# A two-layer hybrid block: paired chunks, masks folded into a matmul, and one convolution tile moved to the end of its section

## The chip, the cores and the metric

The kernel runs on one core of one Trainium2 chip. The metric is device time in microseconds (us) of one execution. The profiled execution is one such run with the hardware profiler on; its span (first to last instruction) is what the rows of a profile add up to.

## What is computed

Two layers over 256 context and 1024 latent tokens of width 1024, one batch. Each layer makes a combined input projection and runs three groups of heads: a bidirectional state-space scan (16 heads of 64, state 128, chunks of 128 tokens), windowed attention, and a convolution module with 31 taps on 512 channels. The change touches the first and the third.

```python
# state space, one direction (the other runs on reversed tokens)
cs = cumsum(dt * a)                       # per chunk of 128 tokens and head
decay = exp(where(tril, cs[l] - cs[s], -inf))
y_diag = (C B^T * decay) @ (x * dt)       # inside a chunk
states = B^T (decay_to_end * x * dt)      # carried from chunk to chunk
y = y_diag + exp(cs) * (C @ entering_state) + D * x
...
# convolution module
h = val * sigmoid(gt)
h = dwconv_31(h)                          # per channel, 31 taps, along the tokens
h = silu(layernorm(h)) @ pw_w
```

## The kernel before

All sequence work is kept as columns: a tile has 128 channels on its partitions and tokens along its free axis. There are ten chunks of 128 tokens, two of context (0, 1) and eight latent (2 to 9). A layer is `ssd_section` (projections for state space and convolution, the scan, the taps), then `att_section`, then `out_section`. The large projections (`gemm1`, tiles `pj`) multiply each weight tile three times, for high and low parts of both operands; they are most of the work of TensorE (PE). The build step orders every engine's queue by a timeline of its own, so a queue runs in a fixed order and each instruction waits at its head.

The scan of a layer is four calls of `half(i, xk)`, each for four heads in both directions. A half has ten steps; step `si` takes the forward chunk `cf` and the backward chunk `cb`, updates the state `S`, and `visit`s each chunk. A chunk's second visit calls `diag(c)`, which makes the decay weights of both directions: the exponents come from matmuls `pc` (forward part and off-diagonal blocks) and `pd` (backward part of the two diagonal 64 by 64 blocks) of `L` (cumulative sums split in three bf16 terms, as rows) with `R` (selectors of heads, and three rows that a DMA brings from `csd`). Triangular masks are added by further matmuls of `identb` with `mask_lt` or `mask_gt`. ScalarE (ACT) takes exponentials into `ex` and `eb`, GpSimd (POOL) adds `eb` into the diagonal blocks of `ex`, VectorE (DVE) multiplies by `cbs`, and PE multiplies `xk` with the result in the same bank in which the chunk's `yp` was transposed; ACT moves the sum out as `yT`. In layer 1 the context chunks have no output, so a half has eight second visits there and ten in layer 0: 72 in all.

Between halves, `conv_gemm(i)` projects convolution channel tile `i` into `gl`; its function `taps` runs `conv31` (one ACT instruction and 30 on DVE for each block of tokens, tile `ua`, result `u`) or, for blocks in `LATER`, stores `gl` to DRAM for the attention section. The rows of `L` are made once per layer before the first half from the tile `qq`.

Of the kernel before, what the change touches and what calls it, by code (L numbers as in the profile page):

```python
# [19 lines left out]
P = 128  # L20
# [35 lines left out]
LATER = (((3, 0), (3, 256), (3, 768)), ((3, 256), (3, 768)))  # L56
STQ = "scalar"
EARLY = 1
SHARE = ((1, 3, 5, 7), (1, 3, 5, 7))
NSM = 4  # L60
# [8 lines left out]
def build(tc, A, out, stop=None, dbg=None):  # L69
# [56 lines left out]
    sel_c = cp.tile([P, 16], BF16, name="sel_c")  # L126
    sel4 = cp.tile([P, 32], F32, name="sel4")
    nc.vector.tensor_reduce(out=sel4[:, 0:16], in_=ident[:, 0:96].rearrange("p (a b) -> p b a", b=16), axis=mybir.AxisListType.X, op=ALU.add)
    nc.vector.tensor_copy(out=sel_c, in_=sel4[:, 0:16])
# [14 lines left out]
    csd = [dp.tile([2, 3, 2, 2, 4, T], BF16, name=f"cs{l}") for l in range(DEPTH)]  # L144
# [401 lines left out]
    def ssd_section(l, last, early):  # L546
        v1 = vec1[l]
        gblocks = LATB if last else ALLB
        with ExitStack() as st:
# [11 lines left out]

            w = load_dt(l)
# [122 lines left out]
            def d1(name, keep=False, dt_=F32):  # L685
                if keep:
                    return sp.tile([P, NCH * 32], F32, tag=name, name=name)
                t = sp.tile([P, 512], dt_, tag="xk", name=name, bufs=7)
                return t[:, 0:NCH * 32]
# [50 lines left out]


            nc.vector.tensor_scalar_mul(out=cs, in0=cs, scalar1=-1.0)
            L = []
            for g in range(2):
                qq = sp.tile([P, NCH, P], BF16, tag=("cbs", "btok")[g], name="qq")
# [4 lines left out]
                for c0, t in ((0, cs), (48, ld)):  # L750
                    x = v4(v3(t))[:, :, :, 8 * g:8 * g + 8]
                    q = [v4(qq[:, :, c0 + 16 * k:c0 + 16 * k + 16]) for k in range(3)]
                    nc.vector.tensor_copy(out=q[0], in_=x)
                    nc.vector.tensor_tensor(out=x, in0=x, in1=q[0], op=ALU.subtract)
                    nc.vector.tensor_copy(out=q[1], in_=x)
                    nc.vector.tensor_tensor(out=q[2], in0=x, in1=q[1], op=ALU.subtract)
                nc.gpsimd.memset(qq[:, :, 96:P], -1.0)
                lt = sp.tile([P, T], BF16, tag=f"L{g}", name="L")
                for b0 in range(0, NCH, 4):
                    nb = min(4, NCH - b0)  # L760
                    pr = pp.tile([P, 1024], BF16, tag="sm", name="pr", bufs=NSM)
                    for c in range(b0, b0 + nb):
# [192 lines left out]
            for i in range(4):  # L955
# [6 lines left out]
                if i == 1:  # L962
                    bc_group(1)
# [524 lines left out]
```

## Time and profile before

| what | value |
|---|---|
| median of 3 runs (lowest to highest) | 2394.25 us (2392.6 to 2397.82) |
| the profiled execution's own time | 2391.2 us |
| its span | 2389.5 us, 36713 instructions |
| PE busy | 2286.8 us, 96% |
| DVE, ACT, POOL busy | 1528.7, 990.3, 1074.5 us |
| granted TensorE clock, mean | 0.985 |

A busy figure is the time in which at least one instruction of the engine was under way. Matmuls overlap at their ends, so PE's work is read from the distance between starts, not from durations. Of the span, the first state-space section takes about 140 to 620 us and the second about 1380 to 1800 us.

### The profile page before, as it was taken

The page shows a single profiled execution, that of the slowest core. Times are in us where ns is not written, and L with a number is a line of the kernel's source. Part 1 is how long each engine was busy: PE and PEld are TensorE (multiplying, and loading weights), DVE is VectorE, ACT ScalarE, POOL GpSimd, SP SyncE. Part 2 cuts the span into 40 slices and gives each one's busy share as a digit, 9 for nine tenths or more (in the row PEclk, how much of TensorE's full clock was granted, in tenths as well). Part 3 has the DMA queues.
Part 4 walks back from the last instruction along what each step waited for, and adds up shares of the span by engine and source line. Part 5 has one row for each costly group of instructions (what it writes and reads, how often), then busy time and mean ns, then how long its engine had stood idle before and what let it go on. Part 6 is the DMA issues. An engine that isn't in the chain of part 4 may idle for free.

```text
span 2389.5 us, 36713 instructions
## 1 busy us (share of the span) xinstructions
PE 2286.8 (96%) x13237; PEld 1813.4 (76%) x13237; DVE 1528.7 (64%) x2738; ACT 990.3 (41%) x2141; POOL 1074.5 (45%) x1249
## 2 busy tenths in 40 slices
PE   6999999999999999999999999999989899998998
PEld 3787678677878777767888787778768676776798
DVE  5779899941266756657363779969323865866534
ACT  6643243322236454544243443343222354554433
POOL 4237663764454323422333346756575532512333
PEclk9999999999999999999999999999999999999999
DMA  7412312333124222247465211111222313226563
GB/s 235 147 59 86 89 49 65 85 101 111 36 83 116 66 72 80 63 152 240 143 201 151 75 41 54 32 41 45 81 54 58 106 58 98 75 71 184 179 177 110
DMA packets 324246, 237.04 MB, mean 99 GB/s; under 512 B 56066, under 2 KB 280546, under 8 KB 324064
## 3 DMA queue, kind: packets, MB, share of 16 engines
q1 hardware_dynamic: 280832, 193.28, 27.5%
q10 hardware_dynamic: 42336, 41.06, 5.5%
q8 instruction: 104, 1.70, 0.3%
q0 software_dynamic: 896, 0.35, 0.1%
q14 instruction: 78, 0.64, 0.1%
HBM read 181.63 MB, written 53.00 MB: 98 GB/s over the span
## 4 chain that ended last, share of the span: by engine, by line
PE 77%; DVE 9%; DMA 6%; ACT 2%; POOL 2%; issue 2%; SPq 1%; ACTq 0%; DVEq 0%; POOLq 0%
PE pj L97 54%; PE sm L97 6%; PE s L97 4%; PE o L97 3%; PE pt L1094 3%; DVE us L513 3%; PE po L97 2%; DMA raw<-oT 2%; PE pc L97 1%; PE pm L97 1%; DMA wr<-w_out 1%; DMA wm<-w_mod 1%; PE sm L917 1%; DVE acc L601 1%; SPq L292 1%
## 5 line engine op out<-in xcount | busy, mean ns | idle before, releaser
L97 PE MATMUL pj<-hh,wh 128*128 128x512 f32 (+1 forms) x1840 | 693.9, 378 | 11.4 <-DVE kb L999 3.3
L97 PE MATMUL pj<-hl,wh 128*128 128x512 f32 (+1 forms) x1840 | 687.2, 373 | 1.6 <-POOL hl L204 1.6
L97 PE MATMUL pj<-hh,wl 128*128 128x512 f32 (+1 forms) x1840 | 686.9, 374 | 1.5 <-POOL wl L423 1.4
L423 POOL TENSOR_TENSOR wl<-wr,wh 128x512 fp32r<-128x512 f32 x268 | 358.1, 1339 | 491.0 <-ACT wh L421 467.0
L97 PEld LDWEIGHTS pj<-hh,wh 128*128 128x128 f32 x1840 | 350.3, 190 | 80.6 <-issue 10.6
L97 PEld LDWEIGHTS pj<-hh,wl 128*128 128x128 f32 x1840 | 349.6, 190 | 61.8 <-issue 6.3
L97 PEld LDWEIGHTS pj<-hl,wh 128*128 128x128 f32 x1840 | 350.5, 191 | 59.8 <-issue 6.8
L421 ACT ACTIVATE wh<-wr 128x512 fp32r<-128x512 f32 x344 | 215.8, 630 | 377.5 <-PE pj L97 288.9
L513 DVE SCALAR_TENSOR_TENSOR ua<-gl,vec,ua 128x512 f32<-128x512 f32 (+1 forms) x435 | 303.2, 697 | 12.0 <-ACT ua L511 5.4
L601 DVE SCALAR_TENSOR_TENSOR acc<-raw,vec,acc 128x514 f32<-128x514 f32 (+2 forms) x280 | 190.4, 692 | 24.2 <-ACT acc L598 22.6
L97 PE MATMUL pj<-ho,wh 128*128 128x256 f32 (+1 forms) x896 | 179.1, 299 | 0.0
L97 PE MATMUL pj<-hx,wh 128*128 128x512 f32 x512 | 166.3, 406 | 10.5 <-DVE hx L505 4.8
L97 PEld LDWEIGHTS pj<-ho,wh 128*128 128x128 f32 x896 | 143.9, 191 | 5.5 <-ACT wh L421 0.2
L938 POOL TENSOR_TENSOR xs<-xk,ws 128x256 f32<-128x256 f32 x144 | 90.4, 639 | 123.2 <-PE sm L97 106.6
L898 POOL TENSOR_TENSOR ex<-ex,eb 64x256 f32<-64x256 f32 x144 | 114.8, 797 | 58.6 <-ACT eb L896 51.4
L1084 ACT ACTIVATE p<-s,sums 128x512 f32<-128x512 f32 (+1 forms) x144 | 95.0, 660 | 102.9 <-DVE sums L1082 82.4
L513 DVE SCALAR_TENSOR_TENSOR us<-gl,vec,us 128x512 f32<-128x512 f32 (+1 forms) x150 | 131.5, 877 | 6.2 <-ACT us L511 4.0
L97 PE MATMUL pj<-ho,wl 128*128 128x256 f32 (+1 forms) x448 | 134.5, 300 | 0.5 <-POOL wl L423 0.3
L1081 DVE TENSOR_REDUCE mx<-s 128x1 f32<-128x512 f32 (+1 forms) x144 | 93.2, 654 | 55.4 <-PE s L97 54.8
L97 PEld LDWEIGHTS pj<-hx,wh 128*128 128x128 f32 x512 | 99.5, 195 | 35.7 <-DVE hx L505 7.2
L912 POOL TENSOR_TENSOR yp<-yp,ye 128x256 f32<-128x256 f32 x136 | 103.3, 776 | 26.8 <-DVE ye L911 26.5
L1094 PE MATMUL pt<-ident,p 128*128 128x128 f32 x640 | 104.0, 278 | 11.7 <-ACT p L1084 7.1
(326 smaller groups left out, 3920.8 us busy)
## 6 DMA issues: line engine op xcount, KB each, us to landing
wr<-w_in SPq DMA_DIRECT2D x160, 256.0 KB
wr<-w_out SPq DMA_DIRECT2D x114, 256.0 KB
wm<-w_mod SPq DMA_DIRECT2D x64, 256.0 KB
raw<-oT ACTq DMA_DIRECT2D x64, 256.0 KB
wr<-w_out SPq DMA_DIRECT2D x76, 128.0 KB
yT<-yT ACTq DMA_DIRECT2D x72, 128.0 KB
wm<-w_mod SPq DMA_DIRECT2D x16, 512.0 KB
wr<-w_in SPq DMA_DIRECT2D x64, 128.0 KB
```

The source lines that it names most:

```text
L97: return nc.tensor.matmul(o, l, r, start=start, stop=stop)
L292: nc.sync.dma_start(out=wm, in_=A["w_mod"][0].rearrange("(k p) c -> p k c", p=P)[:, k:k + 8 // WD, m * P:(m + WD) * P])
L421: nc.scalar.activation(out=hi, in_=raw, func=AF.Copy)
L423: low_eng[0].tensor_tensor(out=lo, in0=raw, in1=f32(hi), op=ALU.subtract)
L513: nc.vector.scalar_tensor_tensor(out=u if t == 30 else acc, in0=g[:, t:t + n], scalar=vec2[l][:, t, j:j + 1], in1=acc, op0=ALU.mult, op1=A ...
L601: nc.vector.scalar_tensor_tensor(out=acc, in0=raw[:, i0 + t:i0 + t + n], scalar=v1[:, cw:cw + 1], in1=acc, op0=ALU.mult, op1=ALU.add)
L898: nc.gpsimd.tensor_tensor(out=e[q, :, q], in0=e[q, :, q], in1=eb[q], op=ALU.add)
L912: nc.gpsimd.tensor_tensor(out=y, in0=y, in1=ye, op=ALU.add)
L938: nc.gpsimd.tensor_tensor(out=h3(xs), in0=xc(c), in1=hb(ws3, c, d), op=ALU.mult)
L1081: nc.vector.tensor_reduce(out=mx, in_=s, axis=mybir.AxisListType.X, op=ALU.min)
L1084: nc.scalar.activation(out=flat(p[:, 0:min(nk, 4), :]), in_=s, func=AF.Exp, scale=-1.0, bias=nm[:, j:j + 1], accum_out=sums[:, 3, j:j + 1])
L1094: last_t[:] = [nc.tensor.transpose(pt[:, q * P:(q + 1) * P], pr[q][:, i, :], ident)]
```

## The change

It has these parts:

- **Masks in the matmul.** `L` gets an identity block in its partitions 64 to 127 and `R` the masks in the same partitions, so one matmul over 128 rows gives a masked exponent. `R` has three versions of its selectors, `pc` is two matmuls of 512 columns, `pd` two of 256, and no mask matmul is left. The fixed parts of `R` and `L` are written by POOL at the start of the section; each half rewrites the selectors with four ACT instructions for each of two `R`.
- **Two chunks at a time.** `diag` becomes `weights(cc)` and `outputs(cc, e)`: both chunks of a step share `ex`, `eb`, `pd`, the transposed bank and `yT`. `outputs` of one pair and `weights` of the next are tied in PE's order by `issue_after`. `ex`, `eb` and `yT` have one buffer where they had two.
- **Scaling of the carried part on ACT.** `ye`, one DVE instruction of 256 columns, becomes four ACT instructions of 64 columns.
- **Rows.** `L` and `csd` are made by `rows()` after `inputs(0)`, five chunks at a time, with 24 small DMAs to `csd` in place of 4, and one `R` load of a chunk in place of two.
- **TAIL.** The taps of channel tile 1 no longer run after `inputs(2)`: `gl` is stored to DRAM, and `tail_taps` loads it again and runs the taps at the end of the section.

```diff
+TAIL = 1
...
+            Rs = []
+            for _ in range(2):
+                R = sp.tile([P, 3, 4, P], BF16, tag="R", name="R", bufs=2)
+                nc.gpsimd.memset(R[32:64], 0.0)
+                nc.gpsimd.memset(R[64:P, 0:2], 0.0)
+                for v, t0, m in ((0, 0, mask_lt), (1, 64, mask_lt), (2, 0, mask_gt), (2, 64, mask_gt)):
+                    nc.gpsimd.tensor_copy(out=R[64:P, v, :, t0:t0 + 64], in_=m[64:P, 64:P].unsqueeze(1).to_broadcast([64, 4, 64]))
+                Rs.append(R)
...
+                        if j == TAIL or (j, off) in LATER[l]:
                             nc.sync.dma_start(out=glTd[l][:, j, u0:u0 + n + 30], in_=gl[:, u0:u0 + n + 30])
...
+            def tail_taps():
+
+                gl = ra("gt")
+                for a, b in ([] if last else [(0, 286)]) + [(286, RA)]:
+                    nc.sync.dma_start(out=gl[:, a:b], in_=glTd[l][:, TAIL, a:b])
+                for off, n in gblocks:
+                    u0 = off if off < CTX else off + 30
+                    conv_taps(TAIL, off, n, gl[:, u0:u0 + n + 30])
...
-                Rs = []
-                for _ in range(2):
-                    R = sp.tile([P, 2, 4, P], BF16, tag="R", name="R", bufs=2)
-                    nc.vector.tensor_copy(out=R, in_=sel4(sel_c).unsqueeze(3).to_broadcast([P, 2, 4, P]))
-                    Rs.append(R)
+                for R in Rs:
+                    for v, d, t0, t1 in ((0, 0, 0, P), (2, 1, 0, P), (1, 1, 0, 64), (1, 0, 64, P)):
+                        nc.scalar.activation(out=R[0:48, v, :, t0:t1], in_=sel_c[0:48, d, 4 * hf:4 * hf + 4].unsqueeze(2).to_broadcast([48, 4, t1 - t0]), func=AF.Copy)
...
-                    mm(pc[:, :, qs[1]], lt[0:99, c * P:(c + 1) * P], r0[:, :, qs[1]], start=True, stop=False)
-                    mm(pc[qs[0], :, qs[0]], ll[0], r0[:, :, qs[0]], start=False, stop=False)
-                    mm(pc[qs[1], :, qs[0]], ll[1], r1[:, :, qs[0]], start=False, stop=False)
+                    with after(last_mm):
+                        for u, (R, c) in enumerate(zip(Rs, cc)):
+                            ll = [lt[:, c * P + a:c * P + a + 64] for a in (0, 64)]
+                            pc = pp.tile([P, 4, P], F32, tag="sm", name="pc", bufs=NSM)
+                            for v, (q, lq) in enumerate(zip(qs, ll)):
+                                mm(pc[q], lq, R[:, v])
+                            for q, lq in zip(qs, ll):
+                                mm(pd[q, u], lq, R[:, 2, :, q])
+                            pcs.append(pc)
+                    for u in range(2):
+                        nc.scalar.activation(out=flat(e[:, u]), in_=flat(pcs[u]), func=AF.Exp)
+                    nc.scalar.activation(out=eb, in_=pd, func=AF.Exp)
                     for q in qs:
-                        mm(pc[q, :, q], identb[:, q], mask_lt[:, q].unsqueeze(1).to_broadcast([P, 4, 64]), start=False, stop=True)
...
-                        mm(pc[q], identb[:, q], mask_gt[:, q].unsqueeze(1).to_broadcast([P, 4, 64]), start=False, stop=True)
...
-                        nc.gpsimd.tensor_tensor(out=e[q, :, q], in0=e[q, :, q], in1=eb[q], op=ALU.add)
+                        nc.gpsimd.tensor_tensor(out=e[q, :, :, q], in0=e[q, :, :, q], in1=eb[q], op=ALU.add)
+                    for u, c in enumerate(cc):
+                        nc.vector.tensor_tensor(out=e[:, u], in0=e[:, u], in1=cbs[:, c, :].unsqueeze(1).to_broadcast([P, 4, P]), op=ALU.mult)
...
-                        nc.vector.tensor_tensor(out=h3(ye), in0=h3(yo), in1=hb(ecs3, c, d), op=ALU.mult)
+                        for h in range(4):
+                            k = 16 * d + H0 + h
+                            nc.scalar.activation(out=ye[:, h * 64:(h + 1) * 64], in_=yo[:, h * 64:(h + 1) * 64], func=AF.Copy, scale=ecs3[:, c, k:k + 1])
...
+                    if si == 2 and not last:
+                        e = weights(steps[1])
+                    if si == 3:
+                        if not last:
+                            outputs(steps[1], e)
+                        e = weights(steps[6])
+                    if si > 6:
+                        outputs(steps[si - 1], e)
+                        e = weights(steps[si])
+                outputs(steps[9], e)
...
+            tail_taps()
             for r in range(NAG[l]):
                 gate_gemm(r)
```

How the queues change is shown at three places. First PE's queue, where one chunk's weights stand in layer 0 before the change (`pc` and `pd` are the exponents, `identb` the mask matmuls; LDWEIGHTS rows are weight loads):

```order
L97 LDWEIGHTS identb
L97 MATMUL pc<-mask_lt,identb 64x4x64
L97 LDWEIGHTS L
L97 MATMUL pd<-R,L 64x4x64
L97 LDWEIGHTS L
L97 MATMUL pd<-R,L 64x4x64
L97 LDWEIGHTS identb
L97 MATMUL pd<-mask_gt,identb 64x4x64
L97 LDWEIGHTS identb
L97 MATMUL pd<-mask_gt,identb 64x4x64
L97 MATMUL pj<-hl_1006,wh 128x512
```

After it, a pair's outputs (`sm<-ex,xk`, two chunks), the next pair's weights behind them, and what PE has until the outputs of that pair; these are the last two pairs of the last half of layer 1 (the rows between `pc` and the second `pd` of the first pair are left away here, they repeat those shown):

```order
L98 MATMUL pd<-R,L 64x256
L98 MATMUL pj<-hh_12695,wl 128x512
L98 MATMUL sm<-S,ct 128x256 x2
L952 MATMUL sm<-ident,yp 128x128 x4
L98 MATMUL sm<-ex,xk 64x128 x8
L98 LDWEIGHTS L
L98 MATMUL pc<-R,L 64x512
L98 LDWEIGHTS L
L98 MATMUL pc<-R,L 64x512
```

```order
L98 MATMUL pd<-R,L 64x256
L952 MATMUL sm<-ident,yp 128x128 x4
L98 MATMUL sm<-ex,xk 64x128 x8
L98 LDWEIGHTS nident
L98 MATMUL s_18483<-mask_gt,nident 128x512
L98 MATMUL pj<-hh_12092,wh 128x512
```

A pair has four `pc` and four `pd` rows and no mask row; `nident` and the `pj` rows behind it belong to the attention section. Between the weights of a pair and its outputs stand here one projection matmul, two of `S` and the transposes, and for the last pair the transposes alone.

DVE's queue at the end of the state-space section of layer 0, after the change (`ua<-gt` are taps of the moved tile, `S` the state update, `ex<-ex,cbs` the multiplication of the weights):

```order
L515 SCALAR_TENSOR_TENSOR ua<-gt,vec_0_391,ua 128x512 x10
L931 TENSOR_TENSOR ex<-ex,cbs 128x512 x2
L515 SCALAR_TENSOR_TENSOR ua<-gt,vec_0_391,ua 128x512
L984 TENSOR_TENSOR S<-S,sm 128x512
L515 SCALAR_TENSOR_TENSOR ua<-gt,vec_0_391,ua 128x512 x9
L931 TENSOR_TENSOR ex<-ex,cbs 128x512 x2
L515 SCALAR_TENSOR_TENSOR ua<-gt,vec_0_391,ua 128x512 x6
L515 SCALAR_TENSOR_TENSOR u<-gt,vec_0_391,ua 128x512
```

Before, this part of DVE's queue holds no taps: only `ye`, `S` and `ex` rows follow each other there. Now the last tap stands ahead of the last pair's `ex` rows.

## Rows read from the trace of the kernel before

**Rows 1.** The page: busy time by engine, and the chain that ended last.

```profile
PE 2286.8 (96%) x13237; PEld 1813.4 (76%) x13237; DVE 1528.7 (64%) x2738; ACT 990.3 (41%) x2141; POOL 1074.5 (45%) x1249
...
PE 77%; DVE 9%; DMA 6%; ACT 2%; POOL 2%; issue 2%; SPq 1%; ACTq 0%; DVEq 0%; POOLq 0%
```

**Rows 2.** Stretches: length, busy PE, PEld, DVE, ACT, POOL, clock, DMA share.

```profile
60.00:95.00 35.00, 32.63 (x175) 27.17 (x175) 24.93 (x48) 24.87 (x53) 7.96 (x16) 0.94 0.58 203
140.00:510.00 370.00, 360.46 (x2311) 279.37 (x2304) 319.89 (x559) 133.63 (x287) 225.71 (x336) 1.00 0.26 75
510.00:620.00 110.00, 103.15 (x618) 79.00 (x617) 30.24 (x58) 30.38 (x62) 58.44 (x71) 0.97 0.33 93
1320.00:1350.00 30.00, 25.82 (x129) 21.48 (x128) 19.66 (x38) 15.63 (x26) 11.15 (x17) 0.89 0.31 97
...
1520.00:1570.00 50.00, 42.60 (x241) 32.62 (x242) 46.64 (x80) 13.20 (x27) 38.87 (x54) 0.93 0.11 30
...
1700.00:1770.00 70.00, 70.00 (x363) 57.28 (x362) 11.77 (x22) 15.91 (x34) 44.81 (x63) 1.00 0.27 77
1770.00:1805.00 35.00, 27.36 (x194) 19.29 (x193) 15.48 (x29) 13.91 (x31) 23.72 (x28) 0.95 0.25 73
```

**Rows 3.** Timeline of PE, one chunk's weights: start, length, instruction.

```profile
302.73 0.51 PE L97 MATMUL pc<-R,L 99*128 99x256 bf16 x3
303.07 0.28 PE L97 MATMUL pc<-mask_lt,identb 128*64 128x256 bf16 x2
303.18 0.28 PE L97 MATMUL pd<-R,L 99*64 99x256 bf16 x2
...
303.50 0.50 PE L97 MATMUL pj<-hh,wh 128*128 128x512 f32 x1
```

**Rows 4.** Timeline of PE: outputs of one chunk alone.

```profile
311.02 0.66 PE L97 MATMUL sm<-ex,xk 128*64 128x128 f32 x8
311.60 0.39 PE L97 MATMUL pj<-hl,wh 128*128 128x256 f32 x1
```

**Rows 5.** Timeline of PE: outputs of two chunks in a row, between projections.

```profile
343.90 0.39 PE L97 MATMUL pj<-hl,wh 128*128 128x512 f32 x1
344.13 0.39 PE L97 MATMUL pj<-hh,wl 128*128 128x512 f32 x1
344.45 1.09 PE L97 MATMUL sm<-ex,xk 128*64 128x128 f32 x16
345.47 0.50 PE L97 MATMUL pj<-hh,wh 128*128 128x512 f32 x1
```

**Rows 6.** Groups by line, shapes apart, of ACT, POOL and DVE: busy, mean ns.

```profile
L889 ACT ACTIVATE ex<-pc 128x512 f32<-128x512 f32 x72 | 43.0, 597 | 104.1 <-PE pd L97 45.4 <-PE pc L97 32.4 <-DMA R<-cs 8.1
...
L1113 ACT ACTIVATE sums<-sums 128x8 f32<-128x8 f32 x18 | 3.8, 209 | 0.4 <-DVE sums L1112 0.4
...
L423 POOL TENSOR_TENSOR wl<-wr,wh 128x512 fp32r<-128x512 f32 x268 | 358.1, 1339 | 491.0 <-ACT wh L421 467.0 <-DMA xb<-xT 8.6 <-DMA wr<-w_out 5.2
...
L513 DVE SCALAR_TENSOR_TENSOR ua<-gl,vec,ua 128x512 f32<-128x512 f32 x348 | 260.8, 750 | 8.5 <-ACT ua L511 4.1
...
L911 DVE TENSOR_TENSOR ye<-sm,ecs 128x256 f32<-128x256 f32 x136 | 51.2, 416 | 65.0 <-PE sm L97 64.8 <-POOL yp L912 0.2
...
L513 DVE SCALAR_TENSOR_TENSOR ua<-gl,vec,ua 128x256 f32<-128x256 f32 x87 | 42.4, 487 | 3.5 <-ACT ua L511 1.3
```

**Rows 7.** Timeline of all engines: the last chunk of layer 1's last half.

```profile
1786.21 0.52 PE L97 MATMUL pc<-R,L 99*128 99x256 bf16 x3
...
1787.37 0.38 ACT L896 ACTIVATE eb<-pd 128x256 f32<-128x256 f32 x1
...
1787.83 1.62 POOL L898 TENSOR_TENSOR ex<-ex,eb 64x256 f32<-64x256 f32 x2 [0.46 <-ACT eb L896]
...
1789.49 0.69 DVE L900 TENSOR_TENSOR ex<-ex,cbs 128x512 f32<-128x512 f32 x1 [1.40 <-POOL ex L898]
...
1790.23 0.33 PE L97 MATMUL sm<-ex,xk 128*64 128x128 f32 x2 [1.43 <-DVE ex L900]
```

More of the change, by code (lines that the diff above doesn't have):

```diff
@@ L143, in build @@
     yTd = [dp.tile([P, KD, T], F32, name=f"yT{l}") for l in range(DEPTH)]
-    csd = [dp.tile([2, 3, 2, 2, 4, T], BF16, name=f"cs{l}") for l in range(DEPTH)]
+    csd = [dp.tile([2, 3, 2, 3, 4, T], BF16, name=f"cs{l}") for l in range(DEPTH)]
     glTd = [dp.tile([P, 4, RA], F32, name=f"glT{l}") for l in range(DEPTH)]
@@ L559, in ssd_section @@
             mod = Modulation([(0, m) for m in range(16, 24, 2)] + [(1, m) for m in range(0, 24, 2)] if l == 0 else [], sp, pt_mod)
+            Rs = []
[6 more added lines that the diff above has]
+                Rs.append(R)
+            L = []
+            for g in range(2):
+                lt = sp.tile([P, T], BF16, tag=f"L{g}", name="L")
+                nc.gpsimd.tensor_copy(out=lt[64:P].rearrange("p (a b) -> p a b", b=64), in_=identb[64:P, 64:P].unsqueeze(1).to_broadcast([64, T // 64, 64]))
+                L.append(lt)
             w = load_dt(l)
@@ L687, in d1 @@
                     return sp.tile([P, NCH * 32], F32, tag=name, name=name)
+                if name in ("s", "cs"):
+                    return sp.tile([P, 512], dt_, tag="u", name=name, bufs=2)[:, 0:NCH * 32]
                 t = sp.tile([P, 512], dt_, tag="xk", name=name, bufs=7)
@@ L742, in ssd_section, with rows @@
             nc.vector.tensor_scalar_mul(out=cs, in0=cs, scalar1=-1.0)
-            L = []
-            for g in range(2):
-                qq = sp.tile([P, NCH, P], BF16, tag=("cbs", "btok")[g], name="qq")
+            nc.vector.tensor_tensor(out=ld, in0=ld, in1=cs, op=ALU.add)
+            def rows():
                 def v4(ap):
                     return ap.rearrange("p c (d j) -> p c d j", d=2)
[L750 to L762, printed above, removed]
-                        nc.tensor.transpose(pr[:, (c - b0) * P:(c - b0 + 1) * P], qq[:, c, :], identb)
-                    nc.scalar.activation(out=lt[:, b0 * P:(b0 + nb) * P], in_=pr[:, 0:nb * P], func=AF.Copy)
-                nc.scalar.dma_start(out=csd[l][g].rearrange("a d f h t -> (a d f h) t"), in_=lt[0:48, :])
-                L.append(lt)
@@ new lines, in half, with weights @@
+                last_mm = []
+                qs = [slice(0, 64), slice(64, P)]
+                def weights(cc):
+                    pcs = []
+                    pd = pp.tile([P, 2, 4, 64], F32, tag="sm", name="pd", bufs=NSM)
+                    e = sp.tile([P, 2, 4, P], F32, tag="ex", name="ex")
+                    eb = sp.tile([P, 2, 4, 64], F32, tag="eb", name="eb")
+                    for R, c in zip(Rs, cc):
+                        nc.scalar.dma_start(out=R[48:51], in_=csd[l][g, :, hf, :, :, c * P:(c + 1) * P])
+                    with after(last_mm):
[10 more added lines that the diff above has]
+                    nc.scalar.activation(out=eb, in_=pd, func=AF.Exp)
+                    for q in qs:
+                        nc.gpsimd.tensor_tensor(out=e[q, :, :, q], in0=e[q, :, :, q], in1=eb[q], op=ALU.add)
+                    for u, c in enumerate(cc):
+                        nc.vector.tensor_tensor(out=e[:, u], in0=e[:, u], in1=cbs[:, c, :].unsqueeze(1).to_broadcast([P, 4, P]), op=ALU.mult)
+                    return e
```

82 lines of the change are left out of this document (43 added, 39 removed).

## The prediction

> **What bounds the kernel now.** I read the page first. PE is busy for 96% of the span and holds 77% of the chain that ended last; DVE, POOL and ACT are at 64, 45 and 41% [rows 1]. So what counts is array time that goes, and PE idle time that goes or comes. Next I read the stretches. Up to 510 us of layer 0's state-space section PE idles 370.0 - 360.5 = 9.5 us, while DVE is busy for 319.9 of 370 us. The idle time of PE sits where the halves end and no projections are left to fill: 6.9 us in 510 to 620, 7.4 us in 1520 to 1570, 7.6 us in 1770 to 1805. DVE is nearly free in the first and the last of these [rows 2]. Third, PE's timeline: a chunk's weights hold the array from 302.73 to 303.50, 0.77 us, and two matmuls of 256 columns that write different partition halves start 0.11 us after the two before them, so they run side by side [rows 3]. One chunk's outputs hold it for 0.58 us [rows 4], two in a row for 1.02 us [rows 5]: the second costs 0.44, and 0.14 is the way in and out. Last, the chain of one chunk where nothing covers it: 1790.23 - 1786.21 = 4.02 us from the first `pc` to the outputs [rows 7].
>
> **The sum, term by term.**
>
> *Array time.* Before, 72 chunks, the count of `ex<-pc` [rows 6], at 0.77 + 0.58 us are 97.2 us [rows 3, 4]. The nine matmuls of a chunk's weights are one at full width and four side-by-side couples, 5 x 0.11 = 0.55, so 0.22 is way in and out. After, a pair of chunks has four `pc` of 512 columns and four `pd` of 256: six couples of 256 columns, 0.66 us. Its outputs cost 1.02 [rows 5], and the next pair's weights follow without a change between, so a pair is 1.68 and 36 pairs are 60.5 us. Not all are joined: the first pair of each half stands alone, and the order shows a dozen pieces with a projection in between; 20 x 0.22 = 4.4. That makes 64.9, and 32.3 us saved. Bounds: 24 if nothing is gained by joining (36 x (1.16 + 0.66 + 0.22) = 73.4), 42 if the ways in and out all go (36 x (0.88 + 0.66) = 55.4). I take 32; the order shows most joins.
>
> *The chain of a pair.* It is longer than that of a chunk, since everything comes in one piece. From 4.02 us [rows 7]: one more exponential of 512 columns, 0.60 [rows 6], and a larger `eb` (0.60 for 0.38), +0.82; weights 0.66 for 0.77, -0.11; POOL's two additions of 512 columns at about 1.34 each, as the nearest shape [rows 6], for 1.62 together, +1.06; the second chunk's multiplication, 0.69, less the 0.44 of outputs that cover it, +0.25. That is 6.0 us, or 5.4 after the weights end. For the last pair of layer 1 the order leaves only transposes as cover, some 0.4 us, and for the one ahead a projection (0.23 us from its start to the next [rows 5]), two matmuls of `S` and transposes, 1.5 us. Of `S` no row shows one alone; the second chunk's outputs, four matmuls of 128 columns in two side-by-side couples, take 0.44 [rows 5], so 256 such columns at full width are an estimated 0.44 each. Counted the same way through the whole order, four more pairs have less than 5.4: 1.3 and 2.4 us at the end of layer 1's second half, 3.1 and 3.6 at the end of layer 0's last. Missing cover: 5.0 + 3.9 + 4.1 + 3.0 + 2.3 + 1.8 = 20.1 us. The other thirty have 6.5 to 25.6 us. In exchange the waits that stand in these three stretches now go, of 21.9 us idle [rows 2] about 16; the rest I put down to loads and to the start of attention. Net +4, with bounds 0 and +20.
>
> *`ye` on ACT.* An ACT instruction of 8 columns takes 0.21 us [rows 6] and one of 256 takes 0.38 [rows 7], so 64 columns are about 0.25 and a `ye` 1.0 us against 0.42 on DVE [rows 6]. 136 of them put 136 us on ACT and take 51 from DVE. ACT is busy for 134 of 370 us where most of them run [rows 2], so they are covered; where that cover is gone, at the six chains, two of them are 1.2 us longer than on DVE. I take +1 (bounds 0 and +7). The Trainium skill's page "ScalarE: Activation LUTs", section "Rules for kernel authors", speaks against this edit: it gives multiplications to VectorE, and puts an ACTIVATE at about 0.3 us and 0.83 ns per element. By that, as an estimate, a `ye` would be 1.4 us, the six chains would pay about 5 us, and the forecast would be 4 us later. The row of 0.21 us for a whole small instruction is below the page's fixed part.
>
> *TAIL.* The taps of tile 1 are 30 x 0.487 + 60 x 0.750 = 59.6 us of DVE in layer 0 and 45 us in layer 1 [rows 6]. They leave the part in which DVE is at 86% and go where it has 79.8 us free of 110 (510 to 620) and 77.7 of 105 (1700 to 1805) [rows 2]. They fit, though in layer 0 with little to spare, since that stretch gets about 7 us shorter. The stores and loads of `gl` go through SP's queue and are hidden: the load is wanted a half later than the store. In the dense part, DVE's relief can give PE back some of its 9.5 us: I take -3, bounds 0 and -10.
>
> *Set-up.* The fixed parts of `R` and `L` are new work of POOL at the start of each section, ahead of `hl` and `wl` instructions in its queue. By POOL's rate for `wl`, 1.34 us per 512 columns [rows 6], eight copies of 256 columns are 5.4 us, two of 1280 are 6.7, and four fills at most 13.4: 12 to 25 us. POOL has 27.0 us free in 60 to 95 and 18.9 in 1320 to 1350 [rows 2]. I take +3 for both layers, bounds 0 and +10. `rows()`, the selectors and the small DMAs are a few us on DVE, ACT and ACT's queue beside projections; half of the `R` loads are gone. I count nothing; uncovered, the 24 small issues would cost some us, once per layer, ahead of the first weights.
>
> Sum: -32 + 4 + 1 - 3 + 3 = -27 us. The profiled execution took 2391.2 us, so 2364; the median of the runs shown is 3 us above it, so 2367.
>
> **Rivals.**
>
> *A. The pair's chain is longer than 5.4 us.* `ex`, `eb` and `yT` have one buffer, the six chains share ACT with weight splits and `ye`, and POOL with `xs` and `yp`. For it: before, POOL was late by itself in these stretches (in the last one DVE waited 1.40 us for it [rows 7]). Against: thirty pairs have a cover over 6.5. At 9 us the six pay 22 more and ten with covers of 6.5 to 8.9 some 12: 34 us, so 2401. Halfway it gives 2384. In long gaps PE also loses its clock: the stretch 1520 to 1570 ran at a mean of 0.93, between 2.4 GHz and some time at 1.2, which is 3.5 us of it, behind waits [rows 2]. The Trainium skill's page "TensorE: Matmul & The Clock Gate", section "Why this matters for your kernels", warns of idle gaps for this reason; six gaps of 3 to 5 us here are longer than the 1.43 there [rows 7]. The rows carry the price without it: the three stretches already run at 0.93 to 0.97.
>
> *B. The moved taps make DVE the last (the other side).* They stand ahead of the last `ex` rows in DVE's queue, in runs of nine and ten (up to 7.5 us) between the state updates. If the stretch needs more of DVE than it has, every late tap holds an `S` or `ex` row, and behind that PE. Wholly uncovered, they cost 59.6 + 45; half of that gives 2367 + 52 = 2419. It decides from 27 us on, a quarter of the taps. Against: DVE's free time there [rows 2].
>
> *C. The time saved on the array is not on the path.* In 140 to 510 DVE is the second bound, at 319.9 us, and a shorter PE would only wait for it; the gain is then about nil, 2390 to 2397. Against: TAIL and `ye` take over 80 us off that very stretch.
>
> *D. The relief is worth more*: all 9.5 us in the dense part, and array time by the upper bound: 2345 to 2352.
>
> **How the numbers follow.** Forecast (2353 to 2381) 0.62; A 0.15, half of it above 2389; B 0.08; C 0.05; D 0.10. A difference under 0.2%, some 5 us, can't be told from none here. Faster: 0.62 + 0.10 + 0.09 = 0.81; same: 0.06 + 0.05 = 0.11; slower 0.08. The range leaves out the best part of D, the worst of A, and B: 2347 to 2391. The likeliest time is 2367 us.
>
> **What would show it.** Right: no mask matmuls, `pc` of 64 x 512 and a `pd` couple 0.11 apart, a joined pair near 1.7 us on the array, PE's busy time lower by about 30 us, six waits of 2 to 5 us before `sm<-ex,xk`, released by DVE's `ex`. DVE less busy in the middle and busier in the last 100 us of each section. Wrong: waits for `ex` or `S` all through the halves (A), waits behind `ua<-gt` and a late first `sh` of attention (B), PE's busy time lower and its idle time higher by as much (C), PE waiting for `wl` or `hl` at the start of a section (set-up).

## The result, and the profile after

The changed kernel takes 2364.43 us (median of four runs, 2362.87 to 2370.22), the kernel before on the same chip 2396.03 us (2392.6 to 2398.52). The ratio is 0.9874, with a 95% interval of 0.9852 to 0.9895: 1.3% faster, well clear of the 0.2% that can be told. The forecast was 2367, in a range of 2347 to 2391.

The page of the changed kernel, busy time by engine and the chain that ended last:

```profile
PE 2252.8 (95%) x12877; PEld 1808.5 (77%) x12877; DVE 1508.2 (64%) x2621; ACT 1126.6 (48%) x2697; POOL 1088.5 (46%) x1209
...
PE 73%; DVE 10%; DMA 4%; ACT 2%; issue 1%; POOL 1%; ACTq 0%; SPq 0%; DVEq 0%; POOLq 0%
```

Against [rows 1] PE has 360 matmuls less and is busy for 34.0 us less; its idle time rose from 2389.5 - 2286.8 = 102.7 to 2361.2 - 2252.8 = 108.4 us. ACT has 136 us more, DVE 20 us less.

Most of this lies in the two state-space sections. To compare kernels I cut each section at the same two instructions, the first transposition by `triu` and the first score matmul of attention. Stretches of the kernel before, cut so (length, then busy PE, PEld, DVE, ACT, POOL, then clock, DMA share and GB/s):

```profile
133.30:684.10 550.80, 533.60 (x3310) 419.15 (x3309) 372.46 (x659) 179.62 (x377) 319.91 (x436) 0.99 0.27 76
1374.70:1869.80 495.10, 478.79 (x2627) 381.27 (x2626) 322.73 (x533) 167.10 (x336) 303.89 (x410) 0.99 0.20 54
```

The same two of the changed kernel, and five others: the set-ups of layer 0 (61 to 96) and layer 1 (1309 to 1339), the dense part of layer 0 that [rows 2] has as 140 to 510 (141.9 to 493.9 here), the making of the rows (147 to 157) and the end of layer 1's section (1752 to 1780):

```profile
61.00:96.00 35.00, 31.14 (x171) 27.26 (x171) 18.51 (x41) 25.93 (x57) 16.16 (x27) 0.92 0.60 211
141.90:493.90 352.00, 337.28 (x2108) 270.04 (x2108) 258.56 (x439) 183.05 (x499) 208.40 (x293) 0.98 0.27 79
135.70:667.50 531.80, 510.31 (x3109) 413.24 (x3108) 358.69 (x597) 246.77 (x659) 309.36 (x399) 0.98 0.28 82
1309.00:1339.00 30.00, 25.74 (x125) 21.15 (x125) 22.08 (x37) 18.42 (x34) 19.55 (x29) 0.89 0.28 85
1362.00:1844.40 482.40, 463.63 (x2467) 379.83 (x2466) 317.44 (x483) 228.99 (x594) 306.96 (x381) 0.98 0.21 58
...
147.00:157.00 10.00, 5.68 (x39) 3.65 (x39) 4.94 (x26) 8.24 (x22) 2.53 (x6) 0.56 0.03 8
...
1752.00:1780.00 28.00, 19.48 (x101) 15.06 (x102) 11.35 (x19) 9.51 (x21) 13.09 (x11) 0.76 0.23 66
```

The sections together went from 1045.9 to 1014.2 us: PE busy for 973.9 instead of 1012.4, idle for 40.3 instead of 33.5. So 38.5 us of array time went, 6.8 us of idle time came. Outside them the kernel has the same matmuls and took 1347.0 instead of 1343.6 us; in the runs below that part varied from 1343 to 1353, so these 3.4 us say nothing about the change. Sum: -38.5 + 6.8 + 3.4 = -28.3 us, the difference of the spans.

Where the array time went is seen in the timeline of PE, one joined piece of the changed kernel (start, length, instruction):

```profile
188.55 1.09 PE L98 MATMUL sm<-ex,xk 128*64 128x128 f32 x16
189.48 0.39 PE L98 MATMUL pc<-R,L 128*64 128x512 bf16 x2
189.69 0.28 PE L98 MATMUL pd<-R,L 128*64 128x256 bf16 x2
189.80 0.39 PE L98 MATMUL pc<-R,L 128*64 128x512 bf16 x2
190.02 0.28 PE L98 MATMUL pd<-R,L 128*64 128x256 bf16 x2
190.23 0.50 PE L98 MATMUL pj<-hh,wh 128*128 128x512 f32 x1
```

Two chunks hold the array from 188.55 to 190.23, 1.68 us, as forecast. In the kernel before, one chunk's weights took 0.77 [rows 3] and its outputs 0.58 [rows 4]. I measured every such piece of both timelines, from its first `pc`, `pd` or `ex` matmul to the next other matmul, less waits: 148 pieces and 103.0 us before, 61 pieces and 69.9 us after, 23 of them whole joined pairs. The other 5.4 of the 38.5 us are in the neighbours: the same 3337 `pj` matmuls of the sections take 6.7 us less. That 87 pieces fewer interrupt them less is a likely reason, but not shown: in before_tail, below, they take 5.6 us less than before with 142 pieces.

The chain of the last pair of layer 1, timeline of all engines of the changed kernel (in brackets the idle time before, and what ended it):

```profile
1756.77 0.64 PE L98 MATMUL pc<-R,L 128*64 128x512 bf16 x2
...
1757.52 0.59 ACT L926 ACTIVATE ex<-pc 128x512 f32<-128x512 f32 x1
...
1758.59 0.60 ACT L926 ACTIVATE ex<-pc 128x512 f32<-128x512 f32 x1 [0.47 <-PE pd L98]
1759.08 0.59 ACT L927 ACTIVATE eb<-pd 128x512 f32<-128x512 f32 x1
1759.75 2.59 POOL L929 TENSOR_TENSOR ex<-ex,eb 64x512 f32<-64x512 f32 x2 [3.36 <-ACT eb L927]
1762.37 1.29 DVE L931 TENSOR_TENSOR ex<-ex,cbs 128x512 f32<-128x512 f32 x2 [6.56 <-POOL ex L929]
1763.12 1.12 PE L98 MATMUL sm<-ex,xk 128*64 128x128 f32 x8 [3.81 <-DVE ex L931]
```

From the first `pc` to the outputs it is 1763.12 - 1756.77 = 6.35 us, against 4.02 for one chunk [rows 7] and a forecast of 6.0. POOL's two additions are its longest step, 2.59 us.

What PE waited for in the changed kernel (total us, times, longest):

```profile
PE sm L98 <- DVE ex L931: 12.9, 6, 3.9
...
PE sm L98 <- DVE S L984: 5.1, 4, 2.7
```

And in the kernel before:

```profile
PE sm L97 <- DVE ex L900: 4.8, 7, 1.4
...
PE sm L917 <- POOL yp L912: 4.4, 4, 2.0
PE sm L97 <- DVE S L946: 4.2, 4, 1.8
```

Six waits for `ex`, three of them of 3.8 to 3.9 us, all three in layer 1; the other three are under 0.5 us. The waits for POOL's `yp` are gone.

### The profile page after: what moved, and what is told of

The parts are those of the page before. It is cut to its first block, busy times and chain, and to the rows that moved or that the text cites. A ratio compares the mean times of both kernels' runs of the same rounds, so it can differ in the third digit from the quotient of the medians.

```text
span 2361.2 us, 36284 instructions
## 1 busy us (share of the span) xinstructions
PE 2252.8 (95%) x12877; PEld 1808.5 (77%) x12877; DVE 1508.2 (64%) x2621; ACT 1126.6 (48%) x2697; POOL 1088.5 (46%) x1209
## 4 chain that ended last, share of the span: by engine, by line
PE 73%; DVE 10%; DMA 4%; ACT 2%; issue 1%; POOL 1%; ACTq 0%; SPq 0%; DVEq 0%; POOLq 0%
PE pj L98 51%; PE sm L98 6%; PE s L98 4%; PE o L98 3%; DVE us L515 3%; DMA raw<-oT 3%; PE pt L1145 3%; PE po L98 2%; DVE ua L515 2%; PE pm L98 1%; DVE ex L931 1%; PE pc L98 1%; DMA wr<-w_out 1%; PE sm L878 1%; DVE acc L619 1%
## 5 line engine op out<-in xcount | busy, mean ns | idle before, releaser
L619 DVE SCALAR_TENSOR_TENSOR acc<-raw,vec,acc 128x514 f32<-128x514 f32 (+2 forms) x280 | 195.6, 712 | 40.8 <-ACT acc L616 38.0
L515 DVE SCALAR_TENSOR_TENSOR ua<-gl,vec,ua 128x512 f32<-128x512 f32 (+1 forms) x290 | 202.7, 699 | 7.4 <-ACT ua L513 1.9
L944 ACT ACTIVATE ye<-sm,ecs 128x64 f32<-128x64 f32 x544 | 119.6, 329 | 90.2 <-PE sm L98 73.0
L929 POOL TENSOR_TENSOR ex<-ex,eb 64x512 f32<-64x512 f32 x72 | 94.7, 1315 | 109.9 <-ACT eb L927 83.8
L945 POOL TENSOR_TENSOR yp<-yp,ye 128x256 f32<-128x256 f32 x136 | 113.3, 842 | 7.1 <-ACT ye L944 6.2
```

Of the source, the lines that this page charges most:

```text
L515: nc.vector.scalar_tensor_tensor(out=u if t == 30 else acc, in0=g[:, t:t + n], scalar=vec2[l][:, t, j:j + 1], in1=acc, op0=ALU.mult, op1=A ...
L619: nc.vector.scalar_tensor_tensor(out=acc, in0=raw[:, i0 + t:i0 + t + n], scalar=v1[:, cw:cw + 1], in1=acc, op0=ALU.mult, op1=ALU.add)
L929: nc.gpsimd.tensor_tensor(out=e[q, :, :, q], in0=e[q, :, :, q], in1=eb[q], op=ALU.add)
L944: nc.scalar.activation(out=ye[:, h * 64:(h + 1) * 64], in_=yo[:, h * 64:(h + 1) * 64], func=AF.Copy, scale=ecs3[:, c, k:k + 1])
L945: nc.gpsimd.tensor_tensor(out=y, in0=y, in1=ye, op=ALU.add)
```

## The experiments

Twelve kernels, all against the kernel before on the same chip. Ratios carry a 95% interval; the kernel before had medians of 2394.2 to 2395.7 us beside them. They ran on several chips, so where a few us decide, ratios are the better comparison: between two kernels they and the medians differ by some 2 us. Six of them make the eight ways to combine three things, with the two kernels of the case: the array edits (masks in the matmul, pairs, rows, set-up), TAIL, and `ye` on ACT.

| kernel | array edits | TAIL | `ye` on | us | ratio to before |
|---|---|---|---|---|---|
| before | no | no | DVE | 2396.0 | 1 |
| before_tail | no | yes | DVE | 2380.9 | 0.9939 (0.9924 to 0.9953) |
| before_ye | no | no | ACT | 2395.9 | 1.0001 (0.9989 to 1.0012) |
| before_both | no | yes | ACT | 2392.7 | 0.9982 (0.9970 to 0.9995) |
| neither | yes | no | DVE | 2393.9 | 0.9992 (0.9978 to 1.0006) |
| ye_dve | yes | yes | DVE | 2391.8 | 0.9981 (0.9971 to 0.9990) |
| no_tail | yes | no | ACT | 2381.0 | 0.9935 (0.9922 to 0.9948) |
| after | yes | yes | ACT | 2364.4 | 0.9874 (0.9852 to 0.9895) |

### TAIL undone

```diff
-TAIL = 1
+TAIL = -1
...
-            tail_taps()
```

> The changed kernel, but the taps of tile 1 stay where they stood before (nothing is taken out to the end of the section). Theory of the prediction: the move is worth 3 us (0 to 10), so this is 2367 (2364 to 2374), with DVE some 45 to 60 us busier in the middle of each section. Rival 1: once PE has lost 38 us of array work, DVE is the next bound in the middle of layer 0, and the move carries much of the gain: DVE would be busy for 304 of 334 us there and the time is 2375 to 2390. Rival 2: the moved taps cost more than they give, by the waits of 3.06 us behind gl and 2.74 us behind S between 470 and 582 us: 2355 to 2361.

Measured: 2380.97 us. Rival 1 is right, the prediction's 3 us are not: in this company the move is worth 16.5 us by the medians, 14.6 by the ratios. The sections of this kernel:

```profile
136.10:678.70 542.60, 516.39 (x3109) 418.43 (x3108) 352.49 (x597) 246.72 (x659) 309.77 (x399) 0.97 0.27 78
1372.40:1860.90 488.50, 465.65 (x2466) 380.40 (x2465) 313.77 (x484) 229.75 (x595) 304.14 (x382) 0.97 0.20 55
```

PE's idle time in them is 49.1 us instead of 40.3, and the same matmuls take 8.1 us longer, at a mean granted clock of 0.97 instead of 0.98.

### `ye` back on DVE

```diff
-                        for h in range(4):
-                            k = 16 * d + H0 + h
-                            nc.scalar.activation(out=ye[:, h * 64:(h + 1) * 64], in_=yo[:, h * 64:(h + 1) * 64], func=AF.Copy, scale=ecs3[:, c, k:k + 1])
+                        nc.vector.tensor_tensor(out=h3(ye), in0=h3(yo), in1=hb(ecs3, c, d), op=ALU.mult)
```

> The changed kernel with ye as one instruction on DVE instead of four on ACT. Theory of the prediction: ACT has cover, the edit costs about 1 us at the short chains, so this is 2363 (2357 to 2366). Rival 1: the four instructions lengthen the six uncovered chains by 1.2 us each, and taking them out gives 7 us: 2357. Rival 2: the 51 us that DVE got rid of matter in the dense part of layer 0, and giving them back costs 5 to 15 us: 2369 to 2379.

Measured: 2391.83 us, 27 us above the changed kernel and beyond every theory's range. An edit that I had priced at a loss of 1 us carries nearly the whole gain, once the rest is there. The sections of this kernel:

```profile
135.00:676.50 541.50, 513.12 (x3109) 415.46 (x3108) 383.03 (x670) 186.82 (x371) 310.43 (x399) 0.98 0.28 81
1371.90:1871.60 499.70, 469.98 (x2466) 383.74 (x2465) 333.94 (x548) 175.80 (x339) 302.72 (x382) 0.96 0.21 56
```

Its group of `ye` (count, then busy us, mean ns, and the idle time of DVE ahead of it):

```profile
L942 DVE TENSOR_TENSOR ye<-sm,ecs 128x256 f32<-128x256 f32 x136 | 51.5, 418 | 54.9 <-PE sm L98 54.1
```

Beside its 51.5 us of work `ye` stood idle at the head of DVE's queue for another 54.9 us, until PE had made its operand, and whatever DVE had queued behind it waited too. PE idles for 58.1 us in the sections, 17.8 more than in the changed kernel; the other 9.2 us of the sections' 27.0 are the same matmuls taking longer, with a mean granted clock of 0.96 instead of 0.98 in layer 1's section. The wait at the head is not the price by itself: in the kernel before `ye` waits longer there, 65.0 us [rows 6], and the same edit gives nothing (below).

### A dummy in place of `ye`

```diff
+                        nc.vector.tensor_tensor(out=h3(sp.tile([P, 256], F32, tag="dm", name="dm")), in0=xc(c), in1=hb(ecs3, c, d), op=ALU.mult)
```

> The changed kernel, ye on ACT as there, with one more instruction on DVE for each ye: the same multiplication of 128x256 by the same factors, but of xk, which has long been there, into a scratch tile that nobody reads. So DVE gets back about the 51 us of work that ye was, but no wait for PE. Theory W (it is the wait: ye stood in DVE's queue until PE had made its operand, 82 us in all where the array edits stand alone, and what stood behind it was late): 2364 to 2372. Rival L (it is the load of 51 us): 2380 to 2395, as with ye itself on DVE (2392).

Measured: 2376.07 us, ratio 0.9918 (0.9907 to 0.9930), between the two. The dummy was even the heavier load:

```profile
L945 DVE TENSOR_TENSOR dm<-xk,ecs 128x256 f32<-128x256 f32 x136 | 77.6, 571 | 5.6 <-ACT xk L880 3.7
```

Neither theory's range holds it. 77.6 us of load with hardly a wait (5.6 us) cost 11.6 us; 51.5 us of load with 54.9 us of waits cost 27.4. So load alone accounts for less than half, and 15 us or more belong to what load doesn't explain: the wait in the queue, or the issue order, which moved too (below).

### Both undone

The last two undone edits, TAIL and `ye`, together.

> The changed kernel without TAIL and with ye on DVE: the array edits (masks in the matmul, pairs, rows, set-up) alone. Theory D: DVE's queue holds the whole array saving up, and undoing the second relief costs little more than undoing the first: 2390 to 2400, as the rival C of the prediction had it. Rival (terms that add up): 2364 + 17 + 27 = 2408 (2402 to 2414). If TAIL and ye were worth only what the prediction gave them, this would be 2364 to 2368.

Measured: 2393.89 us: theory D, and rival C of the prediction to the letter (2390 to 2397). The sections with the array edits alone:

```profile
135.00:681.00 546.00, 517.25 (x3109) 418.51 (x3108) 373.87 (x670) 187.73 (x371) 313.95 (x399) 0.97 0.27 78
1370.50:1867.60 497.10, 466.27 (x2466) 380.93 (x2465) 328.90 (x546) 174.66 (x338) 299.95 (x381) 0.97 0.20 54
```

What PE waited for there:

```profile
PE sm L98 <- DVE ex L931: 13.7, 4, 4.9
PE sm L98 <- DVE S L982: 12.0, 7, 4.3
```

And DVE's group of `ye`:

```profile
L942 DVE TENSOR_TENSOR ye<-sm,ecs 128x256 f32<-128x256 f32 x136 | 51.4, 417 | 82.0 <-PE sm L98 81.7
```

PE's busy time in the sections is 983.5 us, 28.9 below the kernel before, so most of the array saving is there (38.5 in the changed kernel). But PE idles for 59.6 us instead of 33.5: 26.1 of the 28.9 come back as waits, nearly all of them behind DVE (`ex` 13.7 and `S` 12.0 us, against 4.8 and 4.2 in the kernel before). Summed over all tiles, the waits of PE in the sections that DVE ended are 38.6 us here, 35.0 in ye_dve, 29.8 in no_tail and 23.6 in the changed kernel, against 13.5 in the kernel before and 7.9 in before_tail.

### The reliefs without the array edits

The same two edits, made in the kernel before.

> The kernel before with TAIL alone: tile 1's taps through DRAM to the end of the section, nothing else changed. Theory D: DVE's queue is a second bound just behind PE, and taking work out of it pays only once PE's own work has shrunk; so the move that was worth 16.6 us in the changed kernel is worth little here: 2388 to 2396. Rival (terms that add up): it is worth the same 13 to 20 us here: 2376 to 2383. The prediction's own term was 3 us: 2393.

> The kernel before with ye alone on ACT, as four instructions of 64 columns, nothing else changed. Theory D: worth little by itself: 2385 to 2396. Rival (terms that add up): the 27 us that it is worth in the changed kernel show here too: 2364 to 2374. The prediction's own term was a loss of 1 us: 2397.

> The kernel before with both reliefs of DVE, TAIL and ye on ACT, and none of the array edits. So far: TAIL alone gave 13 us, ye alone nothing, the array edits alone nothing. Theory F: ye on ACT pays only with pairs, whose one multiplication of ex per pair is waited for by outputs and by the next weights; so this is TAIL alone again, 2378 to 2383, and the array edits give the other 15 us of the change. Rival G: the two reliefs need only each other, and give the whole gain without any array edit: 2362 to 2370.

Measured: 2380.9, 2395.85 and 2392.67 us. TAIL alone gives 13 to 15 us, as the rival had it; theory D, which gave it next to nothing without the array edits, fell. `ye` alone gives nothing, which is what the prediction's own term said. And the two together give 3 us, not the 13 of TAIL: theories F and G both fell. The sections of before_tail:

```profile
133.90:672.70 538.80, 527.95 (x3309) 415.31 (x3308) 377.69 (x657) 180.08 (x377) 320.11 (x436) 1.00 0.28 80
1367.50:1857.30 489.80, 476.66 (x2627) 382.21 (x2626) 333.45 (x533) 166.53 (x336) 307.20 (x410) 0.99 0.21 57
```

The same of before_both:

```profile
131.20:682.50 551.30, 535.12 (x3310) 420.91 (x3309) 361.13 (x587) 239.85 (x665) 316.68 (x436) 0.98 0.28 79
1377.30:1869.20 491.90, 477.42 (x2627) 381.72 (x2626) 312.54 (x469) 219.34 (x592) 306.75 (x410) 0.99 0.21 56
```

With `ye` on ACT beside TAIL the same matmuls took 7.9 us more than in before_tail and PE idled 6.7 us more, nearly all of it in layer 0, without one wait above 2 us; the mean granted clock of that section is 0.98 instead of 1.00. I have no shown cause for that.

### Pairs undone

```diff
+                            if c in seen:
+                                outputs(c)
...
-                    if si > 6:
-                        outputs(steps[si - 1], e)
-                        e = weights(steps[si])
```

> The changed kernel with the pairs undone: weights and outputs of one chunk at a time, where they stood before, with two buffers of ex, eb and yT; the masks stay in the matmul, and TAIL, ye, rows() and the set-up stay. Theory of the prediction: a chunk holds the array for 0.55 + 0.58 us, 81 to 85 us in all against 70 for pairs and 103 before, and cuts the projections more often; the waits of 12.9 us for ex shrink to about 4. Net +8 to +16: 2372 to 2380, and the gain over before is about half from the masks and half from the pairs. Rival 1: the waits eat what the pairs save: 2360 to 2366. Rival 2: nearly all of the gain is the pairs': 2385 to 2396.

Measured: 2392.67 us, ratio 0.9995 (0.9985 to 1.0005). Rival 2: without pairs nothing is left of the gain. The profiled execution took 2399.7 us, the slowest of the eleven; its sections:

```profile
136.80:688.70 551.90, 530.72 (x3110) 412.08 (x3109) 349.01 (x597) 253.41 (x699) 317.65 (x439) 0.98 0.28 79
1382.50:1877.40 494.90, 475.63 (x2467) 379.02 (x2466) 307.07 (x483) 232.98 (x626) 309.70 (x413) 0.98 0.21 56
```

The pieces themselves take 81.2 us, as forecast, 22 less than before. But PE's busy time in the sections is only 6.0 us lower than before. The timeline has 149 pieces, as many as before, many of them half a chunk's weights; the projections beside them take 7.3 us longer than before, and the mean granted clock of the sections is 0.98 instead of 0.99, where 0.01 of 1047 us is some 10 us of work. PE also idles for 40.5 us instead of 33.5. The kernel before_both, with both reliefs and no array edit, took the same 2392.67 us, so masks in the matmul, rows and set-up give nothing here without the pairs.

### `rows()` ahead of `inputs(0)`

```diff
+            rows()
             xk = inputs(0)
-            rows()
```

> The changed kernel with rows() ahead of inputs(0), where the making of the rows stood before. Theory A: the 5.4 us of PE waits between 147 and 156 us of layer 0 (with the granted clock at 0.58 in 150 to 160) and the 2.7 us at 1396 us of layer 1 are the price of rows() standing behind inputs(0), in the queues of DVE and ACT between the last pieces of acc, raw and xk; with rows() first they go, and the time is 2355 to 2361. Theory B: the same work makes PE wait wherever it stands, or inputs(0) is late in its place: 2362 to 2370, with waits of the same size behind raw, xk or xs instead.

Measured: 2374.71 us, ratio 0.9912 (0.9899 to 0.9925). Theory B in kind, and 4.7 us above its range. Of the waits between 147 and 156 us the one of 1.95 us for `sg` stayed, and those for `raw` and `Q` became one (timeline of this kernel):

```profile
150.74 2.13 PE L785 MATMUL pr<-identb,Q 128*123 128x128 bf16 x15 [5.67 <-ACT Q L781]
```

So moving the rows behind `inputs(0)` is worth some 10 us to the change, and what they still cost there is seen in the changed kernel's timeline:

```profile
148.82 1.33 PE L878 MATMUL sm<-ident,raw 128*128 128x128 f32 x5 [0.80 <-DVE raw L622]
...
151.25 2.13 PE L785 MATMUL pr<-identb,Q 128*123 128x128 bf16 x15 [1.10 <-ACT Q L781]
...
155.33 1.94 PE L98 MATMUL pm<-wm,sc 128*32 128x256 f32 x16 [1.95 <-ACT sg L805]
```

With the 1.57 us at 147.48 that is 5.4 us in layer 0, and one wait of 2.66 us for `sg` in layer 1.

### A control: pairs in the other order

```diff
                 def weights(cc):
+                    cc = cc[::-1]
...
                 def outputs(cc, e):
+                    cc = cc[::-1]
```

> A control: the changed kernel with the two chunks of every pair taken in the other order, in weights and in outputs alike. No work, no tile and no wait is added; the issue order shifts in some places (334 of some 8900 rows of PE differ). Theory: shifts of order that carry no load or relief are worth at most a few us: 2361 to 2368. Rival E: where the pieces come to stand by chance is worth as much as the edits undone so far: 2370 to 2392, and then 10 to 27 us for one undone edit say little about that edit.

Measured: 2368.57 us, ratio 0.9885 (0.9869 to 0.9900), half a us above the theory's range. The order alone is worth some 4 us here, not 10 to 27. Inside, though, layer 0's section got 10.5 us longer (531.8 to 542.3), and the stretch between the sections took 3.8 us of that back, so what a single section shows is less certain than the total. By their traces the kernels with an edit undone differ from the changed one in more places of PE's order than this control does, so it bounds chance only for a smaller shift.

### Half of the additions on DVE, at the short chains

```diff
-                    for q in qs:
-                        nc.gpsimd.tensor_tensor(out=e[q, :, :, q], ...
+                    for q, eng in zip(qs, (nc.gpsimd, nc.vector if short else nc.gpsimd)):
+                        eng.tensor_tensor(out=e[q, :, :, q], ...
...
-                        e = weights(steps[si])
+                        e = weights(steps[si], (i == 1 and si > 8) or (i == 3 and si > 7))
```

> The changed kernel, where in the last pair of the second half and the last two pairs of the last half one of the two additions ex + eb goes from POOL to DVE, which has nothing to do then. Theory: the two run beside each other instead of one after the other, 1.3 us of the chain at each of the three waits of 3.8 to 3.9 us in layer 1 and at the small ones of layer 0: those waits come down to about 2.6, and the time is 2358 to 2362. Rival: DVE and POOL slow each other down (beside a POOL addition the multiplication of ex took 0.92 us a piece, alone 0.65), and the waits stay within half a microsecond: 2363 to 2367.

Measured: 2365.22 us, ratio 0.9873 (0.9860 to 0.9885): no gain, the rival. The last pair's chain shows both theories at work:

```profile
1761.84 0.69 DVE L929 TENSOR_TENSOR ex<-ex,eb 64x512 f32<-64x512 f32 x1 [3.94 <-ACT eb L927]
1761.94 1.71 POOL L929 TENSOR_TENSOR ex<-ex,eb 64x512 f32<-64x512 f32 x1 [4.59 <-ACT eb L927]
1763.68 1.29 DVE L931 TENSOR_TENSOR ex<-ex,cbs 128x512 f32<-128x512 f32 x2 [1.15 <-POOL ex L929]
1764.42 1.98 PE L98 MATMUL sm<-ex,xk 128*64 128x128 f32 x16 [2.94 <-DVE ex L931]
```

Only three pairs were edited, and the wait of 3.94 us in layer 1's second half belongs to one that was not, the pair ahead of the last. POOL's addition, 1.30 us alone (half of 2.59), took 1.71 beside DVE's, so the pair of them took 1.8 instead of 2.59 and the wait fell from 3.81 to 2.94 us, not to 2.6. The Trainium skill's page "SBUF — State Buffer", section "Who interferes with whom", has a likely reason: a VectorE instruction with two SBUF inputs contends with a GpSimd instruction that reads SBUF, for a shared port that one of them holds alone. The trace agrees in kind: POOL's addition took 0.41 us longer. DVE's ran on for 0.59 us after POOL's began, so POOL's was not held up for all of that time. The wait ahead of the last fell by 0.3 us, and a new one of 1.6 us came up.

### Without the rule that joins

```diff
-                            last_mm[:] = [mm(ps[...
+                            mm(ps[...
```

> The changed kernel without the rule that the weights of a pair are issued behind the outputs of the pair ahead. Theory of the prediction: 23 joined pieces of 1.68 us fall apart into 1.03 and 0.88, which costs 0.22 us each, 5 us in all, and some more for projections cut in two: 2366 to 2374. Rival: freed weights start earlier, the chain behind them is covered better, and the waits for ex shrink by more than the array loses: 2354 to 2362.

Measured: 2358.97 us (2355.91 to 2362.52), ratio 0.9847 (0.9834 to 0.9860): the rival, and the fastest kernel of all. Its sections:

```profile
134.10:672.60 538.50, 517.08 (x3110) 412.62 (x3109) 355.61 (x597) 247.62 (x659) 310.84 (x399) 0.98 0.28 81
1363.60:1839.00 475.40, 464.06 (x2465) 378.76 (x2465) 317.32 (x484) 230.82 (x594) 307.25 (x382) 0.98 0.22 59
```

What PE waited for in it:

```profile
PE sm L98 <- DVE ex L931: 5.7, 2, 4.5
PE sm L98 <- DVE S L984: 5.1, 4, 1.7
```

The array does lose what the theory said, 981.1 us against 973.9, but the waits for `ex` fall from 12.9 to 5.7 us, and idle time in the sections falls by 7.5; the last pair's weights start at 1751.40 there, ahead of the outputs before them at 1752.08. In layer 1 the section is 7.0 us shorter (475.4; the changed kernel, the control, rows_first and dve_add all have 482 to 483), which I put down to the edit. In layer 0 it is 6.7 us longer (538.5), but there the order alone makes 532 to 542. So the profiled sections come out equal, and the 3.6 us that this run was shorter outside them don't belong to the edit; the medians differ by 5.5 us and the ranges of the runs don't overlap. So it is better by some 5 us, though the intervals of the two ratios still overlap, from 0.9852 to 0.9860.

## Why the prediction came out right, and where it was wrong inside

**The sum.** Forecast -27 us, measured -28.3 in the profiled execution. Right in kind for the array and in the idle time; wrong in what held the two together. That the total came so close is in part luck: the array gave 6.2 us more than forecast, and 1.8 us more idle time and 3.4 us outside the sections, which say nothing about the change, took most of that back.

**Array time.** Forecast -32.3, with 1.68 us for a joined pair. The pieces lost 33.1 us and a joined pair is 1.68 us. The sections lost 38.5, and I counted only the pieces, not their neighbours. Mis-sized by 6 us, within the stated 24 to 42.

**The chain of a pair.** Forecast 6.0 us and 20.1 us of missing cover at six places. Measured 6.35 us, at the lower clock, and 12.9 us of waits: 3.81 for the last pair (5.0 forecast), 3.85 for the one ahead (3.9), 3.94 for the pair ahead of the last in layer 1's second half (4.1), and little for that half's last (3.0). The two places in layer 0 kept their cover, so of six waits of 2 to 5 us three came. The waits of before that were to go, went in part: idle time in the sections rose by 6.8 us over all, where the terms that touch it summed to +5.

**`ye` on ACT.** This is the step that failed: "136 of them put 136 us on ACT and take 51 from DVE ... I take +1". The load was about right (119.6 us on ACT, below), the price was not. I priced it by the cover on ACT, the engine that takes it, and gave nothing for the queue that it leaves. Its undoing costs 27 us. In the kernel before the same edit is worth nothing, so it is not a gain of its own either: the array saving comes through only beside it.

```profile
L944 ACT ACTIVATE ye<-sm,ecs 128x64 f32<-128x64 f32 x544 | 119.6, 329 | 90.2 <-PE sm L98 73.0 <-POOL yp L945 13.3 <-POOL S L983 3.7
```

The wait for PE is still there (73.0 of the 90.2 us of idle time ahead of `ye`), but now it holds up ACT. One `ye` instruction lasts 329 ns; the Trainium skill's page "ScalarE: Activation LUTs", section "Rules for kernel authors", gives 0.35 as an estimate from its figures, and the trace agrees. They start 0.22 us apart, though (119.6 / 544), so its price in the queue was the lower one.

**TAIL.** "I take -3". Undone it costs 16.5 us, alone it gives 13 to 15, and beside the array edits with `ye` on DVE only 2. I had looked for PE idle time that DVE's relief could give back (9.5 us) and not for the matmuls that run slower between waits: before_tail has 9.5 us less idle time in the sections and 7.8 us less busy time with the same matmuls. The taps did fit at the end, as forecast; rival B did not come.

**Set-up and rows.** Set-up was forecast at +3; POOL needed about 10 us per section, below the 12 to 25 of the prediction, and PE is as busy in 1309 to 1339 as before (25.74 against 25.82 us [rows 2]); in layer 0's set-up, 61 to 96, it idles for 3.9 us against 2.4 [rows 2]. That is some 1.5 us. `rows()` was counted at nothing; ahead of the first weights PE now idles for about 8 us (5.4 + 2.66), where the kernel before has 1.5, and in layer 0 this is a stretch at a granted clock of 0.56, so for the most part at 1.2 GHz. The two errors point opposite ways. The 24 small issues to `csd`, which the prediction has once per layer, are 12 in each; one holds ACT's queue for 0.7 us in the median.

**Rival C** was no rival but a condition. "The time saved on the array is not on the path" is what happens where `ye` stays on DVE: by the medians the array edits give nothing with neither relief (2394 to 2394 in one comparison) and lose 11 us beside TAIL alone. Beside `ye` alone they gain 15 us, beside both 28. The sentence "TAIL and `ye` take over 80 us off that very stretch" decided the case, and I used it as an argument against C where it should have been a term with a price. The figure was too high as well: in that stretch DVE is busy for 258.6 us instead of 319.9 [rows 2], 61 less.

**What stays open.** Why `ye` on ACT costs 10 to 12 us beside TAIL in the kernel before; why its wait there, longer than in ye_dve, is free; how much of the 27 us is the wait in DVE's queue and how much a changed issue order; and why layer 0's section varies by 10 us with the order. Each edit moves the order of all engines, and the one control bounds that at some 4 us for a smaller shift, not for these.

## What to carry to other kernels

When the bound engine gets shorter, ask of every in-order queue that feeds it whether it can follow; here the saving was only there when DVE's could. Look at the work in a queue and at the waits at its head, but neither gave the price by itself: `ye`, with 51 us of work and 65 of waits, was free in the kernel before and cost 27 us here. Terms that are small one by one need not add up: time the array saving with and without each relief, since here +11, 0, -15 and -28 us were the same edits in four companies. And a rule that keeps pieces together on the array also delays what starts the next chain; try it without.

## What the hardware showed that I had not expected

The mean granted clock of the whole run fell from 0.985 to 0.977 (0.972 in ye_dve), though PE was idle for only 6 us more. Where the changed kernel waits several times within a few us, in 147 to 157 and in 1752 to 1780, the rows show 0.56 and 0.76, and `pc` couples 0.64 us long at 1756.77 against 0.39 at 189.48.

The multiplication of `ex` (128x512 on DVE) takes 979 ns in the mean with pairs, 753 ns before and 708 with pairs undone, though it is the same instruction; its median is 716 and its longest 1786. The two that ran with POOL idle, at 1762.37, took 1.29 us together. The trace separates it: 16 of the 72 have no POOL instruction beside them and took 682 to 693 ns each, and every longer one ran beside a POOL instruction. That fits the shared port named above.
